# Layer 1 attention: the scores of both query chunks in one group, their softmax steps spread over later turns

## The chip, the core and the metric

The kernel runs on one core of one Trainium2 chip. The metric is the time of one execution on the device in microseconds (us), the median of several runs. Five engines matter here, each with its own queue of instructions: PE (TensorE: matrix products and transposes), ACT (ScalarE: activations and copies), DVE (VectorE), POOL (GpSimd) and SP (which issues the transfers). Instructions of one engine keep the order in which the program was written; between engines, semaphores make an instruction wait for another.

## The reference

Two decoder layers on x of 256 positions by 1024 features. Each has an attention with 16 heads of 64 and a gated feed-forward part with a short convolution. Layer 0 has a dilated attention in three head groups, layer 1 a block-sparse one. With 256 positions there is one block of 256, so no block is "fully past", and layer 1 comes down to plain causal attention:

```
def mixer_moba(h, w_qkv, q_gain, k_gain, w_o, cos, sin):
    qkv = (h @ w_qkv).reshape(B, S, 3, N_HEADS, HEAD_DIM)
    q = apply_partial_rope(rmsnorm(qkv[:, :, 0], q_gain), cos, sin)
    k = apply_partial_rope(rmsnorm(qkv[:, :, 1], k_gain), cos, sin)
    v = qkv[:, :, 2]
    ...
    s_own = jnp.einsum('hqd,hkd->hqk', qc, k_own).astype(jnp.float32) * ATTN_SCALE
    s_own = jnp.where((kpos[None, :] <= qpos[:, None])[None], s_own, -jnp.inf)
    p = jax.nn.softmax(jnp.concatenate([s_sel, s_own], axis=-1), axis=-1).astype(v_sel.dtype)
    ...
    return out.astype(h.dtype) @ w_o
```

## The kernel before

All large products are float32 products in two parts: a weight tile `raw` is split into `whi` (ACT, L109) and `wlo` (DVE, L117), and three matmuls (L456, L457, L458) make up one product of 128x128 by 128x512. `Stream.pump` does this splitting some units ahead of their use, and each split frees a buffer for the next transfer.

The program is written in **turns**. `turn()` first starts up to two new splits on ACT, then runs the functions that earlier turns have booked in the tables `first` and `pre`, then the turn's own large product (12 matmuls in the attention, 6 in the output projection), and last what is booked in `post`. `at(table, dt, fn, ...)` books a function dt turns later. So a booking sets the place of a step in all engines' queues at once, and on ACT and DVE everything of `first` stands ahead of everything of `pre`.

Layer 1's attention handles four **sections** of four heads each. Their first turns are 0, 8, 12 and 16, counted from the start of this attention (sections 0 and 3 also compute the values, so they have 8 turns); the output projection starts at turn 24. A section has two **chunks** of 128 queries, chunk 0 (128 keys) and chunk 1 (256 keys). For each chunk:

- the products of q and k; ACT squares and copies them (L539, L533); DVE sums, rotates and scales them (`head_sums`, L544 to L556; `factors`, L565); PE transposes them (`transpose`, L580); ACT copies the transposes out (L610) and DVE makes their second parts (`second_parts`, L616 and L618);
- `step_A`: the scores on PE, into the four-buffer PSUM tile `S`. Chunk 0 is 4 small matmuls (L676, each of which the trace counts as two), chunk 1 is 12 (L682). Both work on 64 rows of the array;
- `step_E`: DVE adds the mask and takes row maxima (L708, L715), then ACT takes exponentials (L717) in place, in the two-buffer tile `sm`;
- `step_R`: DVE takes the reciprocals of the sums (L722) and scales the rows (L724);
- `step_T`: PE transposes the weights into `S` (L732);
- `step_V`: ACT copies them to `pT` (L739), which frees that buffer of `S`;
- `step_C`: PE multiplies them with the values (L764, on 64 columns of the array), into the one-buffer tile `O`; one turn later `split_T` copies the result out, on ACT (L444) and DVE (L445), twice each by turns.

Before the change, chunk 1 is booked in two halves of two heads. Scores stand at turns s, s+2 and s+4 of a section with s = 6, 5 or 7; E follows one turn, R and T two turns behind. Value products follow when the last half's weights are there, two turns behind its transposes. In section 3, T stands three turns behind the scores.

Of the kernel before, what the change touches and what calls it, by code (L numbers as in the profile page):

```python
# [10 lines left out]
F32 = mybir.dt.float32  # L11
# [6 lines left out]
P = 128  # L18
# [11 lines left out]
NSEC = NH // HS  # L30
# [8 lines left out]
PUMPS = (0, 0, 0, 1, 1, 1, 1, 1, 1, 1, 1, 1, 1, 0, 1, 1)  # L39

PART_TURNS = 80
PART = {"step_C": 0, "step_A": 1, "step_T": 2, "transpose": 3}

PLANS = (14, 24), (14, 20), (16, 24)

# [13 lines left out]
def r32(ap):  # L59
    return ap.bitcast(F32)  # L60
# [81 lines left out]
def trunk_kernel(ctx, tc, x, a_w_qkv, a_w_o, b_w_qkv, b_w_o, ffn_norm, ffn_w_up, ffn_w_down, pack, mask_a, mask_b,  # L142
# [5 lines left out]
    sp = ctx.enter_context(tc.tile_pool(name="sp", bufs=1))  # L148
# [64 lines left out]
    first, pre, mid, post = {}, {}, {}, {}  # L213

    def at(table, dt, fn, *args):
        table.setdefault(now[0] + dt, []).append((fn, args))

    def turn(fn, pump=2, crowded=False):

        t = now[0]  # L220
        end = len(ws.parts) if t >= LATE else None
        n = min(pump, 1 if len(ws.parts) - ws.taken >= AHEAD else 2)
        if not crowded:
            ws.start(n)
        for f, a in first.pop(t, ()):
            f(*a)
        ws.finish(1, end)
        for f, a in pre.pop(t, ()):
            f(*a)
        if crowded:  # L230
            ws.start(n)
        ws.finish(end=end)
        if fn is not None:
            fn()

        late = post.pop(t, [])
        if t < PART_TURNS:
            late.sort(key=lambda fa: PART.get(fa[0].__name__, len(PART)))
        for f, a in late:
            f(*a)  # L240
        now[0] += 1
# [219 lines left out]
    def attention(xT, norms, ng, g0, mask):  # L461


        dil = ng == 3
# [160 lines left out]
        def v_first(res):  # L625

            def done(c, acc):
                rt = norms[c].r  # L630
                t = res[c][1] if res[c] else new_v()
                res[c] = [bp.tile([P, SW], F32, name="v1", bufs=4), t]
                nc.scalar.activation(res[c][0], acc[:, 0:SW], AF.Copy, scale=rt)
                for a in range(2):
                    r = slice(a * 64, (a + 1) * 64)
                    nc.scalar.activation(t[r, a], acc[r, SW:2 * SW], AF.Copy, scale=rt[r])

            yield from product(done)
# [24 lines left out]
        def step_A(sec, c, heads, qkT, v, rq):  # L663

            n = 3 * P if dil else (c + 1) * P
            cs = slice(c * P, (c + 1) * P)

            banks = [ps.tile([P, 512], F32, name="S", bufs=4) for _ in range(len(heads) if dil else 2)]
            place = [(banks[i], 0) if dil else (banks[i % 2], i // 2 * n) for i in range(len(heads))]
            todo = [(s2, o, slice(h % 2 * HD, h % 2 * HD + HD), h // 2) for (s2, o), h in zip(place, heads)]  # L670
            pairs = [todo[i:i + 2] for i in range(0, len(heads), 2)]
            for two in pairs:
                if not dil and c == 0:
                    t0 = qkT[0][0]
                    for s2, o, rows, pr in two:
                        nc.tensor.matmul(s2[:, o:o + n], r32(t0[rows, 0, pr]), r32(t0[rows, 1, pr]),  # L676
                                         start=True, stop=True)
                    continue
                q, kT = (qkT[0][0][:, :, :, cs], qkT[0][1]) if dil else qkT[0][1:]
                for a, b in ((0, 0), (1, 0), (0, 1)):  # L680
                    for s2, o, rows, pr in two:
                        nc.tensor.matmul(s2[:, o:o + S], q[rows, a, pr], kT[rows, pr, b],  # L682
                                         start=(a + b == 0), stop=(b == 1))
            for two in pairs if dil else ():
                for a in range(2):
                    r = slice(a * 64, (a + 1) * 64)
                    for j in range(2):
                        t = qkT[1 + (a + j) % 2][c]
                        for s2, o, rows, pr in two:
                            oj = o + S + j * 64  # L690
                            nc.tensor.matmul(s2[r, oj:oj + 64], r32(t[rows, 0, pr, r]), r32(t[rows, 1, pr, r]),
                                             start=True, stop=True)
            den, mx, nb_ = (sp.tile([P, 4], F32, name=t, bufs=2) for t in ("den", "mx", "nbias"))
            sm = []
            wide = dil and len(heads) > 2
            for i in (0, 2) if wide else (0,):
                at(pre if i and sec < NSEC - 1 else first, 1, step_E, c, heads, rq, place, n, slice(i, i + 2 if wide else len(heads)), sm, den, mx, nb_)
            at(first, 2, step_R, heads, sm, den, n)
            at(post, (2 if sec == NSEC - 1 else 4) if wide else 3 if not dil and sec == NSEC - 1 else 2, step_T, sec, c, heads, v, sm, n)

        def step_E(c, heads, rq, place, n, part, sm, den, mx, nb_):

            t = bp.tile([P, 768], F32, name="sm", bufs=2)
            these = range(len(heads))[part]
            sm.extend(t[:, i * n:(i + 1) * n] for i in range(len(these)))
            for i in these:
                s2, o = place[i]
                nc.vector.tensor_tensor_reduce(  # L708
                    out=sm[i], in0=s2[:, o:o + n], in1=mask[:, c * moff:c * moff + n],
                    op0=ALU.add, op1=ALU.max, scale=1.0, scalar=-3.0e38, accum_out=mx[:, i:i + 1])  # L710
            if dil:
                nc.vector.tensor_scalar_mul(nb_[:, part], mx[:, part], -1.0)
            else:
                f = rq[c][:, heads[these[0]]:heads[these[-1]] + 1]
                nc.vector.scalar_tensor_tensor(nb_[:, part], mx[:, part], -1.0, f, op0=ALU.mult, op1=ALU.mult)  # L715
            for i in these:
                nc.scalar.activation(sm[i], sm[i], AF.Exp, bias=nb_[:, i:i + 1],  # L717
                                     scale=1.0 if dil else rq[c][:, heads[i]:heads[i] + 1], accum_out=den[:, i:i + 1])

        def step_R(heads, sm, den, n):  # L720
            rd = sp.tile([P, 4], F32, name="rd", bufs=2)
            nc.vector.reciprocal(rd[:, 0:len(heads)], den[:, 0:len(heads)])  # L722
            for i in range(len(heads)):
                nc.vector.tensor_scalar(sm[i], sm[i], rd[:, i:i + 1], None, op0=ALU.mult)  # L724
# [45 lines left out]
        if dil:  # L770
            plan, odd, begin = ([(s, c, (0, 1, 2, 3)) for c, s in enumerate(p)] for p in PLANS)
            last = [(13, 0, (0, 1, 2, 3)), (16, 1, (0, 1, 2, 3))]
        else:
            plan, odd, last = ([(s, 0, (0, 1, 2, 3)), (s + 2, 1, (0, 1)), (s + 4, 1, (2, 3))] for s in (6, 5, 7))
        pumps = PUMPS if dil else (2, 0, 0, 2, 1, 2)
        vs = [[None, None] for _ in range(NSEC)]
        for sec in range(NSEC):
            qk, v, rq = [], vs[sec], {}
            starts.append(now[0])
            for s, c, heads in last if sec == NSEC - 1 else begin if dil and sec == 0 else odd if sec % 2 else plan:  # L780
                at(post, s, step_A, sec, c, heads, qk, v, rq)
            dones = [qk_block(sec, g, qk, rq) for g in range(ng)]
            if dil and sec == 0:
                gens = [opening(dones), product(dones[2], "S")]
            else:
                gens = [product(d) for d in dones]
            gens += [v_first(v)] if dil else []
            gens += [v_last(vs[sec // 2 * 2:sec // 2 * 2 + 2])] if sec in V_TURN[ng] else []
            fns = [fn for gen in gens for fn in gen]
            if sec == 0:  # L790
                fns[0:5] = [fns[i] for i in (range(5) if dil else (0, 1, 4, 2, 3))]
            for i, fn in enumerate(fns):
                turn(fn, pumps[i] if sec == 0 and i < len(pumps) else 2, dil and sec == NSEC - 1 and i > 12)
# [228 lines left out]
    at(post, 12, nc.sync.dma_start, pk[:, 264:PK], pack[:, 264:PK])  # L1022
    at(post, 20, nc.sync.dma_start, mB, mask_b)
    aT = attention(xT, norms, NG, 0, mA)
    for c in range(2):
        nc.gpsimd.dma_start(xr[:, c, :], x[0, c * P:(c + 1) * P, :])
# [17 lines left out]
    at(first, 2, ready, norms2[1])  # L1044
    at(post, 2, warm_table, AF.Exp)
    aT = attention(xT2, norms2, 1, 3, mB)
    xT = new_T()
    out_proj(1, aT, xT)
# [87 lines left out]
```

## Time and profile before

| what | value |
|---|---|
| runs before | 762.38, 762.62, 762.74 us; median 762.62 |
| profiled execution, first to last instruction | 760.9 us (no other time is recorded of it) |
| DVE busy in the span | 582.3 us (77%) |
| ACT busy in the span | 506.0 us (67%) |
| transfers | 133.83 MB, 176 GB/s in the mean |
| layer 1 attention with its first turns of the output projection, 478 to 562 us | PE busy 84.00 of 84.00, DVE 67.87, ACT 61.15 |

A row of the timeline reads: start in us, duration in us, engine, line, operation, tile written <- tiles read, shape, count, and in brackets the idle time of the engine ahead of it with what ended it. Matmuls overlap in the pipeline (a matmul of 512 columns lasts 0.39 us, and the next starts 0.23 us behind it), so the cost of work on PE is read from starts, not from durations.

### The profile page before, as it was taken

Reading aid. Unit: us, or ns where it says so; the run is one execution under the profiler, and the core shown is the slowest. Engines: PE = TensorE matmul, PEld = TensorE weight load, DVE = VectorE, ACT = ScalarE, POOL = GpSimd, SP = SyncE. Lnnn points to the kernel's source line nnn. Section 1 sums busy time; section 2 is a strip of 40 time slices with the busy share of each in tenths; the row PEclk is TensorE's granted clock in tenths of the full one; section 3 lists DMA queues with packets and bytes.
Section 4 is the critical chain, followed back from the end, with each engine's and each line's share of the span. In section 5 each row is a group of like instructions: output and inputs, shape, how many; then the busy total and the mean of one; then the engine's idle time right before and its main releaser. Section 6 shows DMA issues by size and latency. Waiting matters only on the chain.

```text
span 760.9 us, 12046 instructions
## 1 busy us (share of the span) xinstructions
PE 756.4 (99%) x4394; PEld 635.4 (84%) x4394; DVE 582.3 (77%) x1123; ACT 506.0 (67%) x887; POOL 69.8 (9%) x77
## 2 busy tenths in 40 slices
PE   9999999999999999999999999999999999999998
PEld 8888888888888888888888888787778888888886
DVE  6887875975786566997887787978866798877874
ACT  7778666757776457676666656777765677566660
POOL 0330120320131000000000001112000000000000
PEclk9999999999999999999999999999999999999999
DMA  9947462562746436487666553743646368666621
GB/s 293 332 141 251 132 186 80 181 217 65 231 158 223 132 90 194 146 251 215 192 193 183 195 190 116 231 139 112 190 116 185 119 186 247 200 178 200 191 100 56
DMA packets 149452, 133.83 MB, mean 176 GB/s; under 512 B 5904, under 2 KB 134544, under 8 KB 149392
## 3 DMA queue, kind: packets, MB, share of 16 engines
q1 hardware_dynamic: 148816, 130.96, 56.0%
q0 software_dynamic: 576, 2.10, 0.7%
q8 instruction: 34, 0.56, 0.3%
q14 instruction: 26, 0.21, 0.1%
HBM read 131.99 MB, written 1.05 MB: 175 GB/s over the span
## 4 chain that ended last, share of the span: by engine, by line
PE 99%; DVE 0%; issue 0%
PE acc L887 14%; PE acc L456 13%; PE acc L458 13%; PE acc L457 13%; PE acc L890 8%; PE S L940 5%; PE S L941 5%; PE S L942 5%; PE O L887 5%; PE O L890 3%; PE O L764 2%; PE acc L513 2%; PE S L732 2%; PE acc L580 2%; PE S L682 2%; PE O L513 1%
## 5 line engine op out<-in xcount | busy, mean ns | idle before, releaser
L117 DVE TENSOR_TENSOR wlo<-raw,whi 128x1024 fp32r<-128x1024 f32 x236 | 283.5, 1217 | 7.0 <-ACT whi L109 6.6
L109 ACT ACTIVATE whi<-raw 128x1024 fp32r<-128x1024 f32 x236 | 244.3, 1054 | 5.7 <-DMA raw<-in_a_w_qkv_dram 2.3
L456 PE MATMUL acc<-whi,xT 128*128 128x512 f32 x424 | 171.8, 405 | 0.0
L458 PE MATMUL acc<-wlo,xT 128*128 128x512 f32 x424 | 165.8, 391 | 0.0
L457 PE MATMUL acc<-whi,xT 128*128 128x512 f32 x424 | 165.4, 390 | 0.0
L887 PE MATMUL acc<-xT,whi 128*128 128x512 f32 x480 | 119.3, 390 | 0.0
L887 PEld LDWEIGHTS acc<-xT,whi 128*128 128x128 f32 x480 | 88.3, 188 | 17.2
L458 PEld LDWEIGHTS acc<-wlo,xT 128*128 128x128 f32 x424 | 79.6, 188 | 17.5
L456 PEld LDWEIGHTS acc<-whi,xT 128*128 128x128 f32 x424 | 79.7, 188 | 16.8 <-issue 1.2
L457 PEld LDWEIGHTS acc<-whi,xT 128*128 128x128 f32 x424 | 79.9, 188 | 14.7
L318 POOL TENSOR_TENSOR rs_y<-rs_v,mhalf 128x8 f32<-128x8 f32 x32 | 53.7, 1681 | 210.9 <-DVE rs_v L316 208.0
L890 PEld LDWEIGHTS acc<-xT,wlo 128*128 128x128 f32 x480 | 65.5, 190 | 4.7
L940 PE MATMUL S<-whi,kT 128*128 128x512 f32 x174 | 68.2, 392 | 0.0
L941 PE MATMUL S<-whi,kT 128*128 128x512 f32 x174 | 68.1, 391 | 0.0
L942 PE MATMUL S<-wlo,kT 128*128 128x512 f32 x174 | 67.7, 389 | 0.0
L890 PE MATMUL acc<-xT,wlo 128*128 128x256 f32 x480 | 66.9, 282 | 0.0
L911 DVE SCALAR_TENSOR_TENSOR qk<-sm,pk,qk 128x255 f32<-128x255 f32 (+1 forms) x160 | 66.6, 476 | 0.4 <-ACT qk L908 0.3
L900 DVE TENSOR_TENSOR sm<-acc,pT 128x256 f32<-128x256 f32 x60 | 25.4, 423 | 46.9 <-ACT pT L899 46.9
L908 ACT ACTIVATE qk<-sm,pk 128x256 f32<-128x256 f32 x80 | 47.8, 598 | 4.0 <-DVE sm L900 3.7
L924 ACT ACTIVATE kT<-qk 128x512 fp32r<-128x512 f32 x22 | 13.9, 633 | 41.2 <-DVE qk L919 41.2
L887 PE MATMUL O<-xT,whi 128*128 128x512 f32 x160 | 40.2, 393 | 0.0
L942 PEld LDWEIGHTS S<-wlo,kT 128*128 128x128 f32 x174 | 32.7, 188 | 7.0
(167 smaller groups left out, 927.5 us busy)
## 6 DMA issues: line engine op xcount, KB each, us to landing
raw<-in_ffn_w_up_dram SPq DMA_DIRECT2D x80, 512.0 KB, 4.2
raw<-in_a_w_qkv_dram SPq DMA_DIRECT2D x144, 256.0 KB, 4.3
raw<-in_ffn_w_down_dram SPq DMA_DIRECT2D x44, 512.0 KB, 3.8
raw<-in_b_w_qkv_dram SPq DMA_DIRECT2D x48, 256.0 KB, 3.5
raw<-in_a_w_o_dram SPq DMA_DIRECT2D x8, 512.0 KB, 3.8
raw<-in_ffn_w_up_dram SPq DMA_DIRECT2D x16, 256.0 KB, 3.6
raw<-in_b_w_o_dram SPq DMA_DIRECT2D x8, 512.0 KB, 3.8
xr<-in_x_dram POOLq DMA_DIRECT2D x2, 512.0 KB, 5.9
```

Source lines behind the costliest of these rows:

```text
L109: self.nc.scalar.activation(hi, raw, AF.Copy)
L117: self.nc.vector.tensor_sub(lo, self.raw[self.done], r32(hi))
L318: nc.gpsimd.tensor_tensor(y, v, mhalf[:, 0:n], op=ALU.pow)
L456: nc.tensor.matmul(acc, T[:, k, 0, cs], hi, start=first, stop=False)
L457: nc.tensor.matmul(acc, T[:, k, 1, cs], hi, start=False, stop=False)
L458: nc.tensor.matmul(acc, T[:, k, 0, cs], lo, start=False, stop=last)
L887: nc.tensor.matmul(acc, hi[:, k], xT[:, k].rearrange("p j t -> p (j t)"), start=(k == 0), stop=False)
L890: nc.tensor.matmul(acc[:, S:2 * S], lo[:, k], xT[:, k, 0], start=False, stop=(k == 7))
L911: nc.vector.scalar_tensor_tensor(o[:, d:S], u[:, 0:S - d], cw[:, first_tap + b:first_tap + b + 1], o[:, d:S], op0=ALU.mult, op1=ALU.add)
L940: nc.tensor.matmul(o, acts[f][:, 0, cs], hi[:, sl], start=start, stop=False)
L941: nc.tensor.matmul(o, acts[f][:, 1, cs], hi[:, sl], start=False, stop=False)
L942: nc.tensor.matmul(o, acts[f][:, 0, cs], lo[:, sl], start=False, stop=stop)
```

## The change

Only layer 1's attention is written in another order; every instruction of the arithmetic is still there, and layer 0 is unchanged. `step_A` is booked for all four heads of both chunks at the same turn (s = 7; 8 in section 0). The steps behind it start 1 turn later for chunk 0, 2 turns for heads 0 and 1 of chunk 1, and 4 turns for heads 2 and 3; T is one turn behind E (two in section 3). And from turn 80 on, what is booked in `post` is sorted as well: scores, then value products, then transposes.

```diff
-PART = {"step_C": 0, "step_A": 1, "step_T": 2, "transpose": 3}
+PART = {"step_C": 0, "step_A": 1, "step_T": 2, "transpose": 3}, {"step_A": 0, "step_C": 1}
...
-        if t < PART_TURNS:
-            late.sort(key=lambda fa: PART.get(fa[0].__name__, len(PART)))
+        order = PART[t >= PART_TURNS]
+        late.sort(key=lambda fa: order.get(fa[0].__name__, len(order)))
...
-            for i in (0, 2) if wide else (0,):
-                at(pre if i and sec < NSEC - 1 else first, 1, step_E, c, heads, rq, place, n, slice(i, i + 2 if wide else len(heads)), sm, den, mx, nb_)
-            at(first, 2, step_R, heads, sm, den, n)
-            at(post, (2 if sec == NSEC - 1 else 4) if wide else 3 if not dil and sec == NSEC - 1 else 2, step_T, sec, c, heads, v, sm, n)
...
+            for d, i, k in ((1, 0, 2), (3, 2, 2)) if c else ((0, 0, 4),):
+                sm, st = [], []
+                at(first, d + 1, step_E, c, heads[i:i + k], rq, place[i:i + k], n, slice(0, k), sm, st)
+                at(first, d + 2, step_R, heads[i:i + k], sm, st, n)
+                at(post, d + (3 if sec == NSEC - 1 else 2), step_T, sec, c, heads[i:i + k], v, sm, n)
...
-            plan, odd, last = ([(s, 0, (0, 1, 2, 3)), (s + 2, 1, (0, 1)), (s + 4, 1, (2, 3))] for s in (6, 5, 7))
+            plan, odd, begin, last = ([(s, c, (0, 1, 2, 3)) for c in range(2)] for s in (7, 7, 8, 7))
...
-            for s, c, heads in last if sec == NSEC - 1 else begin if dil and sec == 0 else odd if sec % 2 else plan:
+            for s, c, heads in last if sec == NSEC - 1 else begin if sec == 0 else odd if sec % 2 else plan:
```

Three places show what this moves. In all of them the line numbers after the change are 9 higher for the steps E to C (L717 is L725, L732 is L741, L739 is L748, L764 is L773).

On PE, the scores of section 3, before. The first row is chunk 0, the next six are a large product, then come transposes of section 2:

```order
L676 MATMUL S<-t_5945 128x128 x4
L456 MATMUL acc<-whi,xT 128x512
L457 MATMUL acc<-whi,xT 128x512
L458 MATMUL acc<-wlo,xT 128x512
L456 MATMUL acc<-whi,xT 128x512
L457 MATMUL acc<-whi,xT 128x512
L458 MATMUL acc<-wlo,xT 128x512
L732 MATMUL S<-ident,sm 128x128 x4
```

The same place after the change:

```order
L676 MATMUL S<-t_5931 128x128 x4
L682 MATMUL S<-kT,t_5932 128x256 x12
L456 MATMUL acc<-whi,xT 128x512
L457 MATMUL acc<-whi,xT 128x512
L458 MATMUL acc<-wlo,xT 128x512
L456 MATMUL acc<-whi,xT 128x512
L457 MATMUL acc<-whi,xT 128x512
L458 MATMUL acc<-wlo,xT 128x512
L741 MATMUL S<-ident,sm 128x128 x4
```

The 12 score matmuls of chunk 1, which stood in two groups of six in later turns, now stand right behind chunk 0's.

On ACT, the turn whose end holds those scores (turn 23), before: two copies of the split of section 1's value products, the copies of section 3's transposed q and k of chunk 1, two weight splits, two exponentials of section 2 and the copy of section 2's transposed weights:

```order
L444 ACTIVATE xT<-O 128x2x128 x2
L610 ACTIVATE kT<-acc,gqk 128x2x128
L610 ACTIVATE t_5946<-acc 128x256
L109 ACTIVATE whi<-raw 128x1024 x2
L717 ACTIVATE sm,den<-sm,nbias,rs_y 128x256 x2
L739 ACTIVATE pT<-S 128x512
```

and after:

```order
L610 ACTIVATE kT<-acc,gqk 128x2x128
L610 ACTIVATE t_5932<-acc 128x256
L109 ACTIVATE whi<-raw 128x1024 x2
L725 ACTIVATE sm,den<-sm,nbias,rs_y 128x256 x2
L444 ACTIVATE xT<-O 128x2x128 x2
L748 ACTIVATE pT<-S 128x512
```

The two L444 copies moved from ahead of the L610 copies to behind the exponentials, because section 1's value products moved from turn 21 to turn 22.

On DVE, the row scaling of section 1's chunk 0 (reciprocal and four multiplies), which its transposes wait for, before:

```order
L722 RECIPROCAL rd<-den 128x4
L724 TENSOR_SCALAR sm<-sm,rd 128x128 x4
L565 TENSOR_TENSOR qk<-qk,rs_y 128x256
L618 SCALAR_TENSOR_TENSOR kT<-acc,gqk,kT 128x2x128
L616 TENSOR_TENSOR t_5540<-acc,t_5540 128x256
L445 TENSOR_TENSOR xT<-O,xT 128x2x128 x2
```

and after:

```order
L723 SCALAR_TENSOR_TENSOR nbias<-mx,rs_y 128x4
L445 TENSOR_TENSOR xT<-O,xT 128x2x128 x2
L117 TENSOR_TENSOR wlo<-raw,whi 128x1024 x2
L731 RECIPROCAL rd<-den 128x4
L733 TENSOR_SCALAR sm<-sm,rd 128x128 x4
```

The split of section 0's value products (L445) and two weight splits now stand ahead of the scaling, where before they stood behind it.

More of the change, by code (lines that the diff above doesn't have):

```diff
@@ L692, in step_A, with step_E @@
                                              start=True, stop=True)
-            den, mx, nb_ = (sp.tile([P, 4], F32, name=t, bufs=2) for t in ("den", "mx", "nbias"))
-            sm = []
-            wide = dil and len(heads) > 2
-            for i in (0, 2) if wide else (0,):
-                at(pre if i and sec < NSEC - 1 else first, 1, step_E, c, heads, rq, place, n, slice(i, i + 2 if wide else len(heads)), sm, den, mx, nb_)
-            at(first, 2, step_R, heads, sm, den, n)
-            at(post, (2 if sec == NSEC - 1 else 4) if wide else 3 if not dil and sec == NSEC - 1 else 2, step_T, sec, c, heads, v, sm, n)
-        def step_E(c, heads, rq, place, n, part, sm, den, mx, nb_):
+            if dil:
+                sm, st = [], []
+                for i in (0, 2):
+                    at(pre if i and sec < NSEC - 1 else first, 1, step_E, c, heads, rq, place, n, slice(i, i + 2), sm, st)
+                at(first, 2, step_R, heads, sm, st, n)
+                at(post, 2 if sec == NSEC - 1 else 4, step_T, sec, c, heads, v, sm, n)
+                return
+            for d, i, k in ((1, 0, 2), (3, 2, 2)) if c else ((0, 0, 4),):
+                sm, st = [], []
+                at(first, d + 1, step_E, c, heads[i:i + k], rq, place[i:i + k], n, slice(0, k), sm, st)
+                at(first, d + 2, step_R, heads[i:i + k], sm, st, n)
+                at(post, d + (3 if sec == NSEC - 1 else 2), step_T, sec, c, heads[i:i + k], v, sm, n)
+        def step_E(c, heads, rq, place, n, part, sm, st):
+            if not st:
+                st.extend(sp.tile([P, 4], F32, name=t, bufs=2) for t in ("den", "mx", "nbias"))
+            den, mx, nb_ = st
             t = bp.tile([P, 768], F32, name="sm", bufs=2)
@@ L718, in step_E, with step_R @@
                                      scale=1.0 if dil else rq[c][:, heads[i]:heads[i] + 1], accum_out=den[:, i:i + 1])
-        def step_R(heads, sm, den, n):
+        def step_R(heads, sm, st, n):
+            den = st[0]
             rd = sp.tile([P, 4], F32, name="rd", bufs=2)
```

## The prediction

> **What bounds the kernel now.** I read the page's head first, then the chain that ended last.
>
> ```profile
> span 760.9 us, 12046 instructions
> PE 756.4 (99%) x4394; PEld 635.4 (84%) x4394; DVE 582.3 (77%) x1123; ACT 506.0 (67%) x887; POOL 69.8 (9%) x77
> ...
> PE 99%; DVE 0%; issue 0%
> ```
>
> PE is busy for 756.4 of 760.9 us, and the chain that sets the end is PE for 99% of its length. So a step on ACT or DVE costs time only if PE comes to wait for it, and whatever shortens PE's own list of work shortens the run. The number of instructions on PE, DVE and ACT does not change. What can change on PE is what it pays between its instructions, and whether it waits at all.
>
> **What PE pays at a small block.** The timeline of PE between the large products (starts, since matmuls overlap):
>
> ```profile
> 485.42 0.39 PE L458 MATMUL acc<-wlo,xT 128*128 128x512 f32 x1
> ...
> 487.01 0.39 PE L457 MATMUL acc<-whi,xT 128*128 128x512 f32 x1
> ...
> 541.95 0.39 PE L458 MATMUL acc<-wlo,xT 128*128 128x512 f32 x1
> 542.27 0.71 PE L676 MATMUL S<-t 64*128 64x128 f32 x8
> 542.91 0.50 PE L456 MATMUL acc<-whi,xT 128*128 128x512 f32 x1
> 543.25 0.39 PE L457 MATMUL acc<-whi,xT 128*128 128x512 f32 x1
> ...
> 544.18 0.40 PE L458 MATMUL acc<-wlo,xT 128*128 128x512 f32 x1
> ...
> 545.09 0.39 PE L457 MATMUL acc<-whi,xT 128*128 128x512 f32 x1
> ...
> 546.01 0.40 PE L458 MATMUL acc<-wlo,xT 128*128 128x512 f32 x1
> 546.34 0.61 PE L682 MATMUL S<-kT,t 64*128 64x256 f32 x6
> 546.88 0.50 PE L456 MATMUL acc<-whi,xT 128*128 128x512 f32 x1
> 547.22 0.40 PE L457 MATMUL acc<-whi,xT 128*128 128x512 f32 x1
> ```
>
> From 545.09 to 546.01 PE starts four large products, so one costs 0.23 us. From the last product ahead of a block to the second behind it there would be 0.46 us without the block; the rest is the block's price. Chunk 0's scores: 543.25 − 541.95 − 0.46 = 0.84. Half of chunk 1's: 547.22 − 546.01 − 0.46 = 0.75. Transposes (L732, from 544.18 to 545.09): 0.45. A half with transposes right behind it (485.42 to 487.01): 1.13, so the half is 0.68 of that. The entry to a block on 64 rows starts 0.32 or 0.33 behind the last product and the second product behind it starts 0.34 behind the first, instead of 0.23: a price is paid at each edge of a block, whatever stands in it.
>
> What twelve L682 cost in one block is seen in layer 0:
>
> ```profile
> 135.50 0.97 PE L682 MATMUL S<-kT 64*128 64x256 f32 x12
> 136.40 0.30 PE L691 MATMUL S<-t 64*64 64x64 f32 x4
> ```
>
> Twelve take 0.90 from start to next start, six 0.54 (546.34 to 546.88): one more costs 0.06.
>
> **Removed: edges.** After the change a section's scores are one block: 0.84 + 12 x 0.06 = 1.56 us. Before, four chunk 0 blocks (3.36), six halves ahead of transposes (4.08) and two halves alone (1.50) make 8.94 us; after, 4 x 1.56 = 6.24. That saves **2.7 us**. Some value products now stand directly behind scores and ahead of transposes, and a chunk 0 block no longer stands ahead of transposes; by the same rows I estimate 0.3 more for these, **3.0 us** in all. The bounds: 2.7, and 3.4 if every new neighbour saves a full edge of 0.1.
>
> **Moved: the steps on ACT and DVE.** The mask and maxima, exponentials, scaling, copies and the split of the value products each issue what they did before, and each queue holds them in a new order. SP's and POOL's lists of instructions read as before, so transfers are asked for in the same order. I walked the new ACT and DVE lists with durations of before, at each PE instruction that reads their results. Before, PE waited nowhere in this stage. After, five places come out late. The rows of the walk:
>
> ```profile
> 502.75 0.60 ACT L539 ACTIVATE sq<-acc 128x512 f32<-128x512 f32 x1 [0.26 <-PE acc L458]
> 504.91 0.28 DVE L708 CUSTOM_DVE_ANT_0 sm<-S,mB 128x128 f32<-128x128 f32 x1
> 506.13 0.49 ACT L717 ACTIVATE sm<-sm,nbias,rs_y 128x128 f32<-128x128 f32 x1 [2.29 <-DVE nbias L715]
> 508.05 0.45 ACT L610 ACTIVATE kT<-acc,gqk 128x256 fp32r<-128x256 f32 x1
> 509.18 0.42 DVE L565 TENSOR_TENSOR qk<-qk,rs_y 128x256 f32<-128x256 f32 x1
> ...
> 513.87 0.41 DVE L708 CUSTOM_DVE_ANT_0 sm<-S,mB 128x256 f32<-128x256 f32 x1
> 514.75 2.36 DVE L117 TENSOR_TENSOR wlo<-raw,whi 128x1024 fp32r<-128x1024 f32 x2
> 514.93 0.60 ACT L717 ACTIVATE sm<-sm,nbias,rs_y 128x256 f32<-128x256 f32 x1 [1.19 <-DVE nbias L715]
> 517.03 0.15 DVE L722 RECIPROCAL rd<-den 128x2 f32<-128x2 f32 x1
> 517.75 0.42 DVE L565 TENSOR_TENSOR qk<-qk,rs_y 128x256 f32<-128x256 f32 x1
> ...
> 533.50 1.53 PE L764 MATMUL O<-pT,v 128*64 128x128 f32 x24
> 534.96 0.50 PE L456 MATMUL acc<-whi,xT 128*128 128x512 f32 x1
> ...
> 536.88 0.37 ACT L444 ACTIVATE xT<-O 128x256 fp32r<-128x256 f32 x1
> 538.16 0.42 DVE L445 TENSOR_TENSOR xT<-O,xT 128x256 fp32r<-128x256 f32 x1 [0.45 <-ACT xT L444]
> ...
> 539.34 0.48 PE L456 MATMUL acc<-whi,xT 128*128 128x512 f32 x1
> 540.92 0.41 DVE L616 TENSOR_TENSOR t<-acc,t 128x256 fp32r<-128x256 f32 x1
> ...
> 542.15 0.59 ACT L717 ACTIVATE sm<-sm,nbias,rs_y 128x256 f32<-128x256 f32 x1
> 543.32 0.59 ACT L739 ACTIVATE pT<-S 128x512 f32<-128x512 f32 x1
> ```
>
> From them: start of the squares to the first mask 2.16 (502.75 to 504.91); mask to exponentials 1.22 for chunk 0 and 1.06 for half of chunk 1; exponentials 1.92 and 1.17; scaling 1.13 and 0.72; a split L444, L445, L444, L445 by turns 536.88 to 538.58 = 1.70, of which the ACT part lets a next copy start after about 1.2; two weight splits on DVE 2.28; a copy to pT 0.59; L618 and L616 0.82 together.
>
> **Wait 1, section 1's chunk 0 transposes at turn 17.** Chunk 0's maxima now start right behind the scores' turn, and the split of section 0's value products (computed at turn 15) stands ahead of the scaling on DVE, with two weight splits behind it. From the squares of turn 15: 2.16 + 1.22 + 1.92 + 1.70 + 2.28 + 1.13 = 10.4. PE reaches the transposes after the scores (1.56 less 0.2 for an entry already made), the value products (534.96 − 533.50 = 1.46), 24 products (5.5), transposes (0.45) and an entry (0.3): 9.1. Late by 1.3. The transposes one turn on wait for 1.06 + two small steps (0.82) + a weight split (514.75 row: 1.18) + 0.72 = 3.8 against 3.4: 0.4 more. Taken **1.6**, bounds 0.8 and 2.0.
>
> **Wait 2, section 2's scores at turn 19.** One section now takes all four buffers of S at once. The second buffer of chunk 1 holds section 1's transposed weights until their copy (L748), which stands on ACT behind the copies of the transposes, two weight splits and two exponentials. In the same list before, from the product at 539.34 to the end of the exponentials (543.32) is 3.98, and the copy is done at 4.57. PE wants the buffer 12 products later, at 541.95 + 0.32 − 539.34 = 2.93, plus chunk 0's scores (0.64, 542.27 to 542.91): 3.57. Late by **1.0**, bounds 0.8 and 1.3.
>
> **Wait 3, section 3's scores at turn 23.** The same list, and now L444 stands behind the exponentials; on DVE, L618 and L616 stand behind L445. The second part of q is there at 3.98 + 1.70 + 0.82 = 6.5; it is read by the third of the twelve L682, wanted at 3.57 or little later. Late by **2.9**, bounds 2.3 and 3.2. Queued behind L616 are the scaling and all of section 3's softmax, which makes the next.
>
> **Wait 4, section 2's value products at turn 26.** From L616's end: scaling 0.72, chunk 0's mask to exponentials 1.22, exponentials 1.92, scaling 1.13, half of chunk 1's mask to exponentials 1.06, exponentials 1.17, copy 0.59: 7.8. PE, released at the same moment, has ten L682 (0.6), 18 products (4.1), transposes (0.45), edges (0.3) and the eight value products that need only earlier copies (0.8): 6.3. Late by **1.5**, bounds 0.8 and 2.0.
>
> **Wait 5, section 3's first value products at turn 28.** From that copy: scaling and a weight split on DVE, the last half's mask, exponentials, L444 twice, a copy: about 5.3 against 4.3 for the rest of the value products, two transposes and 12 products. **1.1** by the walk, bounds 0 and 1.5.
>
> Together 1.6 + 1.0 + 2.9 + 1.5 + 1.1 = 8.1 us, bounds 4.7 and 10.0. **The sum:** against the profiled execution's span, 760.9 − 3.0 + 8.1 = 766.0. The median of the runs is 1.7 above that span, time around it that the change leaves alone: 762.6 − 3.0 + 8.1 = **767.7 us**. By the bounds, 763.9 (3.4 saved, 4.7 waited) to 769.9 (2.7 and 10.0).
>
> **The rivals.** *It does what it says, and nothing waits.* For it: PE waits nowhere before, and its partners have slack:
>
> ```profile
> L717 ACT ACTIVATE sm<-sm,nbias,rs_y 128x128 f32<-128x128 f32 (+1 forms) x32 | 17.2, 540 | 15.0 <-DVE nbias L715 15.0
> ```
>
> This group of 478 to 562 us shows ACT idle for 15.0 us ahead of exponentials. Against: that idleness is inside the chain mask, exponentials, scaling; it is latency, and the change puts more links into it. Time: 762.6 − 3.0 = 759.6. It decides, and the kernel becomes faster, if the waits sum to less than 3.0. Chance 0.07. *Only waits 2 and 3 bind*, which rest on a buffer and a queue that the order alone fixes, while 1, 4 and 5 are differences of long sums: 762.6 − 3.0 + 3.9 = 763.5. Chance 0.12. *The waits slow the clock as well.* The program's start:
>
> ```profile
> 4.49 2.05 PE L513 MATMUL acc<-whi,xT 128*128 128x512 f32 x4
> ...
> 8.24 1.07 PE L513 MATMUL acc<-whi,xT 128*128 128x512 f32 x4
> ```
>
> The same four matmuls take 2.05 us there and 1.07 later: PE comes out of its first idle time at half speed and changes by 6.3 us, having started at about 1. If wait 3 did that again, some 5 us at half speed would cost 2.6 more: 770.3. Against: it is the only such place, and far more idle time precedes it. Chance 0.08. The Trainium skill, "TensorE: Matmul & The Clock Gate", section "What's actually happening", asks for a whole idle window of about 3.4 us before the rate falls; by that rule 2.9 us would not do, and the time would stay 767.7; no row here has an idle time of this length.
>
> **How the numbers follow.** The forecast has 0.73. The range reaches down to the rival with two waits and up to the bound of the waits: 763.3 to 769.9; below it lies the first rival, above it the slowed clock. A measurement of this kernel tells 0.2%, 1.5 us, from no change, so "same" is 761.1 to 764.1: it holds most of the two-wait rival and the forecast's lowest end. Faster 0.07, same 0.12, slower 0.81.
>
> **What would show it.** Right: PE's busy time falls, and its timeline has idle time ahead of L741 at turn 17 (released by DVE's scaling), inside L682 at turns 19 (ACT's pT) and 23 (DVE's L616), and inside L773 at turns 26 and 28; the largest at 23. Blocks of scores cost 1.56. DVE and ACT busy stay at 582 and 506. Wrong: no idle ahead of these, which would mean that the lists run closer together than the walk; or blocks that cost as much as before, which would mean that edges are not what the small blocks pay for.

## The result and the profile after

| | us, median | runs | ratio to before, 95% interval |
|---|---|---|---|
| before | 762.62 | 762.38 to 762.93 | |
| after the change | 768.17 | 767.92 to 769.52 | 1.0075 (1.0065 to 1.0086) |

The change makes the kernel slower by 5.6 us; 767.7 us were forecast. The profiled execution has a span of 766.4 us. Its page, the lines that answer to those shown of before:

```profile
span 766.4 us, 12047 instructions
PE 756.2 (99%) x4394; PEld 635.8 (83%) x4394; DVE 581.9 (76%) x1123; ACT 506.3 (66%) x887; POOL 69.5 (9%) x77
...
PE 94%; DVE 3%; ACT 2%; DMA 1%; issue 0%; SPq 0%; ACTq 0%; DVEq 0%
```

DVE and ACT do the same work in the same busy time. The chain that ended last no longer runs on PE alone: 5% of it is now on DVE and ACT. PE's busy time has hardly fallen, though its blocks of scores cost less; the reason is found below (matmuls that wait inside their group, and a stretch at half clock).

The view of waits of PE in the changed kernel (who waited for whom, us in total, times, the longest):

```profile
PE S L682 <- ACT pT L748: 3.0, 2, 2.0
PE S L269 <- DVE qk L266: 1.0, 1, 1.0
PE O L773 <- DVE rd L731: 0.9, 1, 0.9
PE S L741 <- DVE sm L733: 0.8, 1, 0.8
PE S L682 <- DVE t L616: 0.3, 1, 0.3
```

L269 is the program's start and stands in the kernel before as well. The other lines hold the waits 1, 2, 3 and 5 of the forecast; the two for L748 are those at turns 19 and 23. The releasers are the ones named there, except at wait 5: the walk ended with ACT's copy, which ends at 559.75, and the view names DVE, whose L445 ends at 559.72, so both were done at the same time. Wait 4 is missing. Where they stand, from PE's timeline:

```profile
517.66 0.92 PE L741 MATMUL S<-ident,sm 128*128 128x128 f32 x4 [0.82 <-DVE sm L733]
...
527.11 0.98 PE L682 MATMUL S<-kT,t 64*128 64x256 f32 x11 [1.00 <-ACT pT L748]
...
543.01 0.72 PE L676 MATMUL S<-t 64*128 64x128 f32 x8
543.48 0.36 PE L682 MATMUL S<-kT,t 64*128 64x256 f32 x1
545.85 0.38 PE L682 MATMUL S<-kT,t 64*128 64x256 f32 x1 [2.01 <-ACT pT L748]
546.54 1.10 PE L682 MATMUL S<-kT,t 64*128 64x256 f32 x10 [0.32 <-DVE t L616]
547.58 0.79 PE L456 MATMUL acc<-whi,xT 128*128 128x512 f32 x1
548.17 0.63 PE L457 MATMUL acc<-whi,xT 128*128 128x512 f32 x1
548.60 0.63 PE L458 MATMUL acc<-wlo,xT 128*128 128x512 f32 x1
...
553.60 1.53 PE L773 MATMUL O<-pT,v 128*64 128x128 f32 x24
555.06 0.65 PE L741 MATMUL S<-ident,sm 128*128 128x128 f32 x4
...
559.86 0.66 PE L773 MATMUL O<-pT,v 128*64 128x128 f32 x8 [0.94 <-DVE rd L731]
```

At turn 23 (543 to 548) the first score of chunk 1 starts at 543.48, the second waits for the buffer until 545.85, and the third for the second part of q until 546.54. And then the large products start every 0.43 us (548.17 to 548.60), not every 0.23. The windows of PE around it (busy and count, granted clock, DMA share, GB/s) tell why:

```profile
545.00:547.00 2.00, 0.83 (x7) 0.99 0.00 0
547.00:549.00 2.00, 2.00 (x11) 0.50 0.03 8
549.00:551.00 2.00, 2.00 (x9) 0.65 0.08 10
551.00:553.00 2.00, 2.00 (x10) 1.00 0.92 285
```

The granted clock is halved from about 547.0 to 550.4: that is the rival to which the prediction gave 0.08, at the place that it named. But the time is the forecast's, not that rival's. And not every execution shows it: of the five, two had a mean granted clock of 1.000 (767.92 and 768.17 us), two of 0.997 (768.17, the profiled one, and 768.36) and one of 0.995 (769.52). What became of the slow clock is the first question for the experiments; whether the waits are the whole loss, and the block edges the whole gain, are the others.

How the waits come about is read from ACT and DVE at turn 23 of the changed kernel (L725 is L717 of before; the lines of `step_E` are 8 higher, those of the steps behind it 9):

```profile
542.90 0.59 ACT L725 ACTIVATE sm<-sm,nbias,rs_y 128x256 f32<-128x256 f32 x1
...
544.06 0.37 ACT L444 ACTIVATE xT<-O 128x256 fp32r<-128x256 f32 x1
544.92 0.38 ACT L444 ACTIVATE xT<-O 128x256 fp32r<-128x256 f32 x1 [0.49 <-DVE xT L445]
545.20 0.59 ACT L748 ACTIVATE pT<-S 128x512 f32<-128x512 f32 x1
...
545.34 0.42 DVE L445 TENSOR_TENSOR xT<-O,xT 128x256 fp32r<-128x256 f32 x1 [0.45 <-ACT xT L444]
...
546.07 0.42 DVE L616 TENSOR_TENSOR t<-acc,t 128x256 fp32r<-128x256 f32 x1
```

PE's second score starts as the copy to pT ends (545.79), the third as L616 ends (546.49). Neither step waits for its own data: the copy stands on ACT behind two weight splits, two exponentials and the two L444, and L616 stands on DVE behind the two L445, which wait for these L444.

### The profile page after: what moved, and what is told of

Its sections match the earlier page's. It is cut to its first block, busy times and chain, and to the rows that moved or that the text cites. A ratio compares the mean times of both kernels' runs of the same rounds, so it can differ in the third digit from the quotient of the medians.

```text
span 766.4 us, 12047 instructions
## 1 busy us (share of the span) xinstructions
PE 756.2 (99%) x4394; PEld 635.8 (83%) x4394; DVE 581.9 (76%) x1123; ACT 506.3 (66%) x887; POOL 69.5 (9%) x77
## 3 DMA queue, kind: packets, MB, share of 16 engines
HBM read 131.99 MB, written 1.05 MB: 174 GB/s over the span
## 4 chain that ended last, share of the span: by engine, by line
PE 94%; DVE 3%; ACT 2%; DMA 1%; issue 0%; SPq 0%; ACTq 0%; DVEq 0%
PE acc L896 14%; PE acc L456 12%; PE acc L458 12%; PE acc L457 12%; PE acc L899 7%; PE S L949 5%; PE S L950 5%; PE S L951 5%; PE O L896 5%; PE O L899 2%; PE acc L513 2%; PE O L773 2%; PE S L741 2%; PE acc L580 2%; PE S L682 1%; ACT sm L725 1%
## 5 line engine op out<-in xcount | busy, mean ns | idle before, releaser
L445 DVE TENSOR_TENSOR xT<-O,xT 128x256 fp32r<-128x256 f32 x16 | 8.3, 522 | 43.0 <-ACT xT L444 43.0
```

## The experiments

Two theories were set against each other. **Theory 1** is the prediction's: each wait comes from what stands ahead of one step in one queue, and the merged blocks save their edges whatever the waits are. (The expectations take 3.2 us for this saving, from 5.55 us lost against 8.8 us of waits and slow products. The slow products were counted 0.2 too high in that; with 8.6 it is 3.0 to 3.1 us.) **Theory 2**: ACT and DVE have no room in this stage, so that what is taken away at one place comes back at another. All kernels compute the whole result. The kernel before, timed beside them, had medians of 762.66 to 762.73 us.

### One copy moved ahead (copy_first)

```diff
-            at(pre, 1, step_V, sec, c, heads, v, Tp, tot)
+            if dil:
+                at(pre, 1, step_V, sec, c, heads, v, Tp, tot)
+            else:
+                first.setdefault(now[0] + 1, []).insert(0, (step_V, (sec, c, heads, v, Tp, tot)))
```

> The changed kernel, with one step moved: in layer 1 the copy of transposed weights to pT is written at the head of its turn, ahead of the exponentials on ACT instead of behind them. Theory 1 (each wait comes from what stands ahead of one step in one queue; the merged blocks save about 3.2 us whatever the waits are): the wait at turn 19 (1.4 us) goes; the one at turn 23 stays at 2.9 us, since the second part of q (DVE, behind the split of the value products) is late by itself, only its first part, released by pT, disappears; the waits at turns 17 and 28 stay (1.7 and 1.0). 766.8 us. Theory 2 (ACT and DVE have no room in this stage, so a wait taken away at one place comes back at another): 768.2 us, as the changed kernel.

Measured: 767.77 us, ratio 1.0068 (1.0055 to 1.0080), a miss for theory 1 by 1.0 us. The wait at turn 19 fell from 1.4 to 0.5 us, but the one at turn 23 grew from 2.9 to 3.4. ACT and PE there:

```profile
542.53 0.60 ACT L751 ACTIVATE pT<-S 128x512 f32<-128x512 f32 x1
543.01 0.60 ACT L725 ACTIVATE sm<-sm,nbias,rs_y 128x256 f32<-128x256 f32 x1
...
544.18 0.38 ACT L444 ACTIVATE xT<-O 128x256 fp32r<-128x256 f32 x1
...
546.66 1.44 PE L682 MATMUL S<-kT,t 64*128 64x256 f32 x10 [3.10 <-DVE t L616]
```

The copy now stands ahead of the exponentials and L444, and L616 hangs on L444. PE reached turn 23 earlier (its block at 542.64 instead of 543.01) and the release came as late as before (546.66, 546.54). The expectation had counted the copy's gain and forgotten what it pushes back in the same queue. Here theory 2's sentence holds, by a mechanism that theory 1 knows. The half clock stands behind this wait too: the four executions with a mean granted clock of 0.997 or 0.998 took 767.75 to 768.16 us, the one with 1.000 took 767.14. So part of the miss may be the slow clock; a single execution does not show it.

### PE kept busy in the longest wait (fill)

```diff
-            for two in pairs:
+            for two in pairs * (5 if not dil and c == 0 and sec == NSEC - 1 else 1):
                 if not dil and c == 0:
```

> The changed kernel, with section 3's chunk 0 scores computed five times over into the same places (16 more small matmuls, about 1.8 us on PE, ahead of the matmul that waits at turn 23). PE is then idle for about 1.1 instead of 2.9 us there. Theory 1 with the half clock hidden (from turn 23 on ACT and DVE set when section 3's first value products can start, so that PE's half speed behind the wait costs nothing): 768.2 us within 0.5; the clock stays whole behind turn 23, and in place of slow products PE waits about 1.5 us at section 2's value products (turn 26), as the forecast's wait 4. Rival (the half clock costs what it adds to the products, about 1.8 us): 766.4 us.

Measured: 768.01 us, 1.0072 (1.0059 to 1.0084). With less idle time at turn 23 the clock stays whole, at the same place and with the same columns as above:

```profile
547.00:549.00 2.00, 1.99 (x15) 1.00 0.00 0
549.00:551.00 2.00, 2.00 (x12) 1.00 0.00 0
```

and wait 4 is there, in section 2's value products, behind the sixteen (the prediction counted eight) that need only earlier copies:

```profile
552.58 1.09 PE L773 MATMUL O<-pT,v 128*64 128x128 f32 x16
554.79 0.66 PE L773 MATMUL O<-pT,v 128*64 128x128 f32 x8 [1.12 <-ACT pT L748]
```

PE has 1.8 us more to do and no slow stretch, and the time is the changed kernel's within 0.2 us. So from turn 23 to section 3's first value products the queues of ACT and DVE set the time; PE's half clock filled a wait that was due anyway. The changed kernel's own executions agree as far as the clock fell no more than in the profiled one. The one whose mean clock was lowest, 0.995, took 1.2 to 1.4 us more than those at 0.997. It has no trace, so that a longer slow stretch is the reason is not shown.

### Exponentials behind copies, splits moved (exp_behind, exp_behind2)

In exp_behind the exponentials are booked in `pre` behind the copies to pT, and the splits of sections 0 and 1 in `pre`; exp_behind2 adds the branch for section 2 and the third piece:

```diff
+            def step_X():
                 for i in these:
                     nc.scalar.activation(sm[i], sm[i], AF.Exp, ...)
+            if dil:
+                step_X()
+            else:
+                at(pre, 0, step_X)
...
-                    at(first, 1, split_T, aT, sec * 2, 2, c, O[sec, c][:, c], dil)
+                    if not dil and sec == 2:
+                        first.setdefault(now[0] + 1, []).insert(c, (split_T, args))
+                    else:
+                        at(pre if not dil and sec < 2 else first, 1, split_T, *args)
...
-                turn(fn, ..., dil and sec == NSEC - 1 and i > 12)
+                turn(fn, ..., sec == NSEC - 1 and (i > 12 if dil else i == 7))
```

> The changed kernel, with ACT's exponentials of layer 1 written behind the copies to pT of the same turn, and the split of sections 0 and 1's value products behind the second parts and one weight split. No instruction is added or removed, and PE's list is that of the changed kernel. Theory 1: wait at turn 17 goes (row scaling no longer behind the split and two weight splits, late by less than 0), at turn 19 0.2 left, at turn 23 about 1.3 (the copy to pT, behind two weight splits and the split of the value products), turn 28 about 1.4: in all about 3.2, as much as the blocks save: 762.6 us, within 1. Theory 2: 766 to 768 us.

> As exp_behind, and two steps more: at turn 23 ACT starts its two weight splits last, and section 2's value products are split first in their turn. Theory 1: nothing waits at turns 17 and 23, 0.2 at 19, 0.7 at 26, about 0.4 at 27 and 28: 1.3 in all against 3.2 saved: 760.7 us, faster than both kernels. Theory 2: 766 to 768 us.

Measured: 763.61 us, 1.0010 (1.0001 to 1.0019), and 762.89 us, 1.0003 (0.9994 to 1.0012). The order of ACT's and DVE's lists alone takes back 4.6 and 5.3 us, with PE's list untouched. exp_behind came out 1.0 above theory 1's number, at the edge of its range, and exp_behind2 2.2 above; theory 2's 766 to 768 us was missed by both. The transposes at turn 17 start without idle time in both, and at turn 23 nothing waits in exp_behind2. Its waits, in a view as above:

```profile
PE O L779 <- ACT pT L754: 1.4, 2, 0.8
...
PE S L747 <- DVE sm L739: 0.6, 1, 0.6
PE S L747 <- DVE mx L716: 0.2, 1, 0.2
```

They sit at turns 20 and 26 to 29, each behind a place from which a wait was taken.

### A first mending that failed, and blocks set apart (exp_behind3, apart)

exp_behind3 moves weight splits (last in their turn at turn 19 too, and other numbers in OUT_ORDER, the count of splits started in each turn of the output projection), and makes one copy to pT in the turn of its transposes:

```diff
-             ((1, (0, 0)), (1, (0, 1)), (1, (0, 2)), (1, (0, 3)), (1, (1, 0)), ... (1, (1, 1)),
+             ((0, (0, 0)), (1, (0, 1)), (0, (0, 2)), (0, (0, 3)), (2, (1, 0)), ... (2, (1, 1)),
...
-            at(pre, 1, step_V, sec, c, heads, v, Tp, tot)
+            if not dil and sec == 2 and heads[0] == 2:
+                step_V(sec, c, heads, v, Tp, tot, 2)
+            else:
+                at(pre, 1, step_V, sec, c, heads, v, Tp, tot)
...
-                turn(fn, ..., sec == NSEC - 1 and (i > 12 if dil else i == 7))
+                turn(fn, ..., sec == NSEC - 1 and (i > 12 if dil else i in (3, 7)))
```

apart is exp_behind3 with:

```diff
-            for d, i, k in ((1, 0, 2), (3, 2, 2)) if c else ((0, 0, 4),):
+            for d, i, k in ((0, 0, 2), (2, 2, 2)) if c else ((0, 0, 4),):
...
-            plan, odd, begin, last = ([(s, c, (0, 1, 2, 3)) for c in range(2)] for s in (7, 7, 8, 7))
+            plan, odd, begin, last = ([(s + c, c, (0, 1, 2, 3)) for c in range(2)] for s in (7, 7, 8, 7))
```

> As exp_behind2, with three steps more on ACT: the two weight splits of turn 19 are started last as well, the splits of turns 24, 26 and 27 are made two and four turns later, and the last copy of section 2's weights to pT is written in the turn of its transposes. PE's list is that of the changed kernel. Theory 1: of the 3.3 us of waits that exp_behind2 still shows (0.5 at turn 20, 1.1 at 26, 0.2, 0.7 and 0.8 at 27 to 29) about 0.3 at turn 27 and 0.4 at turn 28 are left, so that nearly all of the 3.2 us that the merged blocks save stands: 760.2 us, within 0.6, faster than the kernel before by 0.3%. Theory 2 (no room on ACT and DVE, what is taken away comes back): 762.5 to 763 us, as exp_behind2.

> As exp_behind3, but chunk 1's scores stand one turn behind chunk 0's in all four sections, with the steps behind them at the turns that they had. So the four merged blocks are eight again, and nothing else is asked of PE. If the merged blocks save their edges, each section pays about 0.4 us again (a chunk 0 block of 0.84 and a chunk 1 block of 0.75 + 6 x 0.06 = 1.11 against 1.56 merged), in two of the four with a neighbour that shares an edge: 1.2 to 1.6 us more than exp_behind3 (761.4 to 761.8 us by its forecast), less what the later reading of the second part of q relieves. Rival (edges cost nothing, the gain is elsewhere): the time of exp_behind3 within 0.3.

Measured: 763.48 us, 1.0009 (1.0000 to 1.0018), and 763.78 us, 1.0015 (1.0006 to 1.0024). Both expectations of theory 1 failed, and exp_behind3 stands 0.5 above theory 2's range too. In exp_behind3 a new wait had come:

```profile
PE S L747 <- DVE mx L716: 1.1, 1, 1.1
```

The weight splits set last at turn 19 delayed ACT's squares of that turn, DVE's head sums wait for these, and the masks behind them in DVE's list free the buffer that turn 20's transposes need. With such waits left, blocks set apart cost little: 0.3 us. What PE pays more at an edge it waits less behind: the wait above is 0.7 instead of 1.1 in apart. But 0.3 us is also what the rival allowed, so this pair alone does not tell whether edges cost anything.

### Nothing in the way (exp_behind4, apart4)

exp_behind4 takes exp_behind3's step at turn 19 back (one weight split there instead), moves other splits, and writes both ACT copies of a value product's split ahead of both DVE parts, where L444 had waited for L445:

```diff
+    def split_two(dst, k0, srcs):
...
+        for hi, lo, s in todo:
+            nc.scalar.activation(hi, s, AF.Copy)
+        for hi, lo, s in todo:
+            nc.vector.tensor_sub(lo, s, r32(hi))
...
-             ((1, (0, 0)), (1, (0, 1)), (1, (0, 2)), (1, (0, 3)), (1, (1, 0)), ... (1, (1, 1)),
+             ((0, (0, 0)), (0, (0, 1)), (1, (0, 2)), (0, (0, 3)), (2, (1, 0)), ... (2, (1, 1)),
```

apart4 is exp_behind4 with apart's two lines.

> As exp_behind2, with the order on ACT and DVE mended where exp_behind2 and exp_behind3 still show PE waiting: one weight split instead of two at turn 19 (the other follows at turn 21), the weight splits of turns 24, 25 and 27 made later, the last copy of section 2's weights to pT in the turn of its transposes, both ACT copies of a value product's split ahead of both DVE parts, and the splits of section 3 behind one weight split. PE's list is that of the changed kernel. Theory 1 (each wait comes from what stands ahead of one step in one queue, and none has to be there): 0.7 us of waits are left of 3.3 in exp_behind2, and most of the 3.2 us that the merged blocks save stands: 760.2 us, faster than the kernel before by 0.3%. Theory 2 (no room on ACT and DVE): 762.5 to 763.5 us, as the three kernels before it.

> As exp_behind4, but chunk 1's scores one turn behind chunk 0's, so that the four merged blocks are eight again. In exp_behind3 against apart PE's blocks cost 0.3 to 0.4 us more for each section apart, but waits behind them took most of it up. If few waits are left in exp_behind4, the edges must show in the time: 1.2 us more than exp_behind4, within 0.4. If the edges are not what the merged blocks save: the same time within 0.3.

Measured: exp_behind4 **759.68 us**, ratio 0.9961 (0.9949 to 0.9974); apart4 761.21 us, 0.9981 (0.9971 to 0.9990). exp_behind4 beats both kernels: 3.0 us less than before, 8.5 less than the changed kernel. Its page and its view of waits:

```profile
span 758.1 us, 12052 instructions
...
PE 99%; DVE 0%; issue 0%
...
PE S L269 <- DVE qk L266: 1.0, 1, 1.0
```

Of PE's matmuls only the first of the program still waits, with all the merged blocks of the change. One of PE's weight loads (PEld in the view) waits near the stage's end, and the products around it come 0.3 us late:

```profile
555.79 0.19 PEld L465 LDWEIGHTS acc<-whi,xT 128*128 128x128 f32 x1 [0.27 <-DVE xT L453]
```

So ACT and DVE had room: theory 2 falls, and that copy_first gained little and exp_behind3 nothing is explained by the waits that were still there. And with almost no wait to absorb it, setting the blocks apart costs 1.5 us by the medians. PE's timeline in section 0, the changed kernel (merged) and then apart4:

```profile
484.48 0.39 PE L458 MATMUL acc<-wlo,xT 128*128 128x512 f32 x1
484.80 0.71 PE L676 MATMUL S<-t 64*128 64x128 f32 x8
485.26 0.96 PE L682 MATMUL S<-kT,t 64*128 64x256 f32 x12
486.15 0.50 PE L456 MATMUL acc<-whi,xT 128*128 128x512 f32 x1
486.49 0.40 PE L457 MATMUL acc<-whi,xT 128*128 128x512 f32 x1
```

```profile
484.82 0.71 PE L684 MATMUL S<-t 64*128 64x128 f32 x8
485.47 0.50 PE L464 MATMUL acc<-whi,xT 128*128 128x512 f32 x1
...
488.10 0.39 PE L466 MATMUL acc<-wlo,xT 128*128 128x512 f32 x1
488.42 0.97 PE L690 MATMUL S<-kT,t 64*128 64x256 f32 x12
489.32 0.50 PE L464 MATMUL acc<-whi,xT 128*128 128x512 f32 x1
489.66 0.40 PE L465 MATMUL acc<-whi,xT 128*128 128x512 f32 x1
```

Merged, the block costs 486.49 − 484.48 − 0.46 = 1.55. Apart, the second block alone costs 489.66 − 488.10 − 0.46 = 1.10, and the first 0.85: 0.4 more. In the three other sections a chunk 1 block has a small neighbour with which it shares an edge, and the difference is about 0.35 each: 1.45 in all, against 1.5 by the medians. (The two profiled executions differ by 1.1 only, since the late weight load of exp_behind4 does not wait in apart4.)

## Why the prediction was right

**The gain.** Forecast 2.7 us from merged scores and 0.3 from new neighbours. exp_behind4 is 3.0 us below the kernel before. PE shows it too: the product behind section 3's first value products starts at 555.12 before and at 552.06 in exp_behind4, with the same work done, and up to there PE waits nowhere in this stage in either, so the edits to ACT's and DVE's lists cannot be what saves it. apart4 shows by experiment that edges make 1.5 us of it, those between chunk 0's block and chunk 1's. The other half, from joining chunk 1's two halves and from the new neighbours, is read from PE's starts alone; no run sets the halves apart. The price of a merged block, worked out as 1.56 from layer 0's twelve matmuls, was 1.55.

**The waits.** The price of each block in the changed kernel less the price of the same block in exp_behind4, where PE does not wait at these places, both from starts as in the prediction. At turn 23 the idle time is told apart: the third L682 could have started at about 543.6 and did at 546.54. The slow clock is the rest: from the last product ahead of the block to the second behind the next transposes it is 8.32 us in the changed kernel (542.69 to 551.01) and 3.84 in exp_behind4 (539.74 to 543.58), 4.48 more, of which 2.9 is the idle time.

| | forecast | measured |
|---|---|---|
| 1, turns 17 and 18 | 1.6 | 1.3 + 0.4 |
| 2, turn 19 | 1.0 | 1.4 |
| 3, turn 23 | 2.9 | 2.9 idle |
| slow clock behind it | none | 1.6 |
| 4, turn 26 | 1.5 | none; 1.35 in fill |
| 5, turn 28 | 1.1 | 1.0 |
| sum | 8.1 | 8.6 |

The sum less the 3.0 saved is 5.6 us, as measured. Waits 1, 3 and 5 came out where and as large as walked. Wait 2 was mis-sized by 0.4: the prediction gave PE 0.64 for chunk 0's scores on the way to the buffer, a figure that holds an edge back to 128 rows; no such edge stands there in the merged block, where chunk 1's first score starts 0.46 to 0.47 behind chunk 0's (543.01 to 543.48), and the rest is the list on ACT.

**What was missed.** The clock fell behind wait 3, which the prediction held unlikely, and wait 4 did not appear. These are one thing: the slow clock brought PE 1.6 us later to section 2's value products, a wait of 1.5 was forecast there, and fill shows 1.35 when the clock stays whole, with the same time. So the total came out although the profiled execution lacks one of the five waits. The rival with the slow clock was right in its mechanism and wrong in its price of 2.6 us more: it added the slow products to the sum and did not ask which later wait they use up. Its counter-argument, that far more idle time precedes the program's start, rests on no row: inside the span PE is idle there for 1.05 us. In wait 4, PE's share was counted wrong: eight value products at 0.8, where fill shows sixteen, about 1.0 by the rate of 24 in 1.46; with them the walk gives 1.3, nearer to the 1.35. That the rival "nothing waits" was forecast at 759.6 us, and exp_behind4 measured 759.68, shows that its number was right for a kernel whose lists are in another order.

## What to carry to other kernels

A merge that saves PE its edges pays only if each result that PE reads is still ready in time; walk the queue of each feeding engine, one instruction after the other, to every such reader, and count what a step moved ahead pushes back. A wait that is taken away shows in the time only when no later wait of the same queues takes it up: judge edits on the last wait of a chain, or with all of them gone. The same holds for a cost, even a halved clock: where a chain on other engines has a wait in store, it can cost as little as what exceeds that wait.

## What the runs showed of the hardware

In the profiled execution of the changed kernel the clock of PE fell to half (by the windows, from 547.0 us) behind idle times of 2.01 and 0.32 us with one matmul between them, and in that of copy_first behind one wait of 3.1 us; in fill, whose longest wait was 1.1 us in this stage, it did not fall. It stayed at half for about 3.4 us (547.0 to 550.4). The Trainium skill, "TensorE: Matmul & The Clock Gate", section "What's actually happening", gives an idle window of about 3.4 us for the fall and as long a busy stretch for the rise. The rise agrees with the trace; the fall came after less, so the prediction's use of that rule failed in this execution. The two executions of the changed kernel with a mean granted clock of 1.000 had the same lists of instructions and kept the clock, so these runs give no length of wait from which it falls.

An L444 waited 0.49 us for the L445 of the other chunk, though they read and write different places of the same tiles. The wait is for a semaphore, so it is the program that orders them. Written as two copies and then two subtractions, both ACT copies were through 0.53 us after the first began (exp_behind4, 538.05 to 538.58), instead of 1.14 (544.06 to 545.20).
